# Four layer norms in a two-layer decoder step: the shifted subtraction and all row sums on VectorE, the convolution's history behind the first group's norm

## The chip, the cores and the metric

The kernel runs on one core of one Trainium2 chip. The metric is device time in microseconds (us). Each version is timed in several runs, of which the median is given; beside these one execution is recorded by the hardware profiler, and all times of single instructions come from that one. Engines: PE is the matrix engine (TensorE), PEld its weight loads, DVE is VectorE, ACT is ScalarE, POOL is GpSimd, SP is the engine that issues most DMA transfers. On-chip memory has two parts: SBUF, and PSUM, whose banks receive the results of matmuls.

## The reference

One inference step of a hybrid decoder with two layers, model width 1024, for a new sequence of 512 tokens and 8 single tokens that continue cached sequences. Layer 0 mixes tokens by sliding-window attention, layer 1 by gated linear attention. After each mixer comes a gated feed-forward network with a causal convolution of width 3, and after each of the four sublayers a normalisation of the sum of input and sublayer:

```python
def layer_norm(x, g, b):
    mu = jnp.mean(xf, -1, keepdims=True)
    var = jnp.mean(jnp.square(xf - mu), -1, keepdims=True)
    return (xf - mu) * lax.rsqrt(var + LN_EPS) * g + b

def conv_ffn(x, buf, w_up, conv_w, conv_b, w_down):
    h = x @ w_up
    a, u = h[..., :D_FF], h[..., D_FF:]                  # gate and value, D_FF = 2816
    ap = jnp.concatenate([buf, a], axis=1)               # two rows of history ahead
    c = conv_b + sum(conv_w[j] * ap[:, j:j + T] for j in range(CONV_W))
    return (gelu(c) * u) @ w_down, ap[:, T:]

for i in range(2):
    x = layer_norm(ALPHA * x + mixer_i(x), ln_mix_g[i], ln_mix_b[i])
    f, new_buf = conv_ffn(x, buf, ffn_w_up[i], ffn_conv_w[i], ffn_conv_b[i], ffn_w_down[i])
    x = layer_norm(ALPHA * x + f, ln_ffn_g[i], ln_ffn_b[i])
```

The outputs are the activations, the new keys and values, the new linear-attention states and the new convolution history.

## The kernel before

**Tiling.** Activations stay on the chip, transposed: 128 partitions of features, 8 chunks (`KD = 8`) of the width, tokens along the free dimension. The 520 tokens go as two groups: `a` with 256 tokens, `b` with 264 (256 of the sequence and the 8 single ones). Weights and activations are float32, split into a high and a low part for the matrix engine, so that a product of one weight unit (a 128-column slice of a weight matrix) with one group is three matmuls of each of 8 chunks: high by high (L238), high by low (L240), low by high (L242). Such a product fills one PSUM bank, a tile named `accp`; there are four of these, and a product can start only when the reader of the product four places earlier has emptied its bank. Weight units arrive by DMA in a tile `raw`; ACT makes the high part `wh` (L196), DVE the low part `wl` (L202), or in the feed-forward phases ACT and a DMA issued by POOL (L207, L208).

**A norm.** There are four norms: norm 0 behind the attention, at about 127 to 186 us of the profiled span, norm 1 behind the first feed-forward network (465 to 530 us), norm 2 behind the linear attention (700 to 770 us), norm 3 at the end (1040 to 1092 us). Each is made for group `a` and for group `b`, and group `b`'s products run on PE while group `a` is normalised. `ln_chunk` is called for each of the 8 output chunks, as its product comes: DVE adds the product to the scaled residual (L343 behind the mixers; L337 with a bias behind the feed-forward networks), which empties the product's bank. Behind chunk 0 a matmul with ones gives the mean of that chunk alone (L347), ACT copies it into SBUF in one or two scalings (`sb`, L349; `sa`, L353), and this shift is subtracted from all eight chunks (L356) before the other products are added, so that the later sum of squares is of small numbers. Chunk 0 is subtracted by DVE and chunks 1 to 7 by POOL, one instruction each, so that chunk m's L343 waits for POOL's m-th subtraction. Then ACT squares each chunk (L361), and the sums over the chunks are gathered in `s1` (L373) and in `s2` (L374). Who adds is set by two limits, `p1, p2`: for group `a`, and for both groups in the last norm, DVE adds into `s1` and POOL adds the first three squares into `s2` (m from 1 to 3, `S2P = 4`), DVE the rest; for group `b` in norms 0 to 2 POOL adds all of both but the last. `ln_end` reduces `s1` and `s2` over the partitions by matmuls (L381), has DVE subtract the rest of the mean in pairs of chunks (L403), computes the reciprocal root, and scales each chunk (L441); ACT and DVE then split the result into its high part `xh` (L442) and low part (L443; for group `a` both sit in the tile `xs_a`), which the next products read.

**The feed-forward network's start.** `ffn_open` runs when the first weight unit of the phase is loaded, well ahead of the norm. It issues the DMA of the convolution's history (`sconv`, L760) on ACT's queue, and has POOL compute from it `base`, the history's share of the convolution for the 8 single tokens, in five instructions (L776 to L780). `base` is read by DVE in `ffn_gate` for group `b` (L810). The first four pairs of gate and value units go one by one: `ffn_gate` makes the convolution's taps (L804 on ACT, L805 and L806 on DVE) and the gelu (L815), `ffn_value` multiplies by the value product (L823), which empties that product's bank, and splits the result. When group `b`'s norm ends, the row sums for the next norm are prepared on DVE (L477 to L488).

**The order of the work.** The program is written as a list of slots: each slot is one product of one group, with what belongs to it. Work that should come later is put on a heap with a number of slots to wait (`spawn`, drawn by `due` after each slot). A scheduler with a timeline simulation then sets the order of the instructions on each engine from their dependences and its own costs, so that a change in one place can move instructions in others; `issue_after` adds an order between two instructions. At run time each engine works through its own list in order.

## Time and profile before

| | |
|---|---|
| median of 3 runs | 1097.64 us (1096.99, 1097.64, 1100.53) |
| profiled execution | 1094.2 us, of which the span of instructions is 1092.5 us |
| PE busy | 1059.4 us, 97% of the span |
| DVE busy | 871.7 us, 80%, 1813 instructions |
| ACT busy | 683.4 us, 63% |
| POOL busy | 319.8 us, 29%, 512 instructions |

The profile's page gives the busy time of each engine. Other views used below: the list of waits (which instruction waited for which, with total, times and longest), the timeline of one engine (start and duration of each instruction, with the idle time before it and what ended that), the table of stretches (busy time of each engine in each), the instructions of one source line (duration as least, median and longest), and the chain of waits that leads to the end. A row of the timeline such as "x4" merges four instructions in a row of one kind; its duration is then that from the first start to the last end. A duration includes the time until the result is written, so the next instruction starts before it is over.

### The profile page before, as it was taken

What the parts mean: (1) busy time and instruction counts of PE and PEld (TensorE: products, weight loads), DVE (VectorE), ACT (ScalarE), POOL (GpSimd) and SP (SyncE); (2) the same over time, 40 slices, a digit from 0 to 9 for tenths busy, and PEclk for the clock granted to TensorE, in tenths of its full rate; (3) what the DMA queues carried; (4) which work ended last, traced back from release to release, by engine and by line L of the source; (5) the groups of instructions that cost most, each with busy time, mean ns of one, the idle gap of its engine ahead of it and who ended that gap; (6) DMA issues with size and microseconds to landing.
All of it is one profiled execution on the core that took longest, in us unless ns stands there. A gap on an engine that the chain in (4) does not pass through costs nothing. (4 is left out here: it accounts for less than half of the span.)

```text
span 1092.5 us, 23877 instructions
## 1 busy us (share of the span) xinstructions
PE 1059.4 (97%) x9174; PEld 1030.2 (94%) x9174; DVE 871.7 (80%) x1813; ACT 683.4 (63%) x1356; POOL 319.8 (29%) x512
## 2 busy tenths in 40 slices
PE   8999999999999999999999999989999999999996
PEld 8998899999999999999899999889999999999995
DVE  7898668988778878978767676588988788778975
ACT  5677657776655665547566656468776655665643
POOL 4576572221111110274321111363221111110263
PEclk9999999999999999999999999999999999999998
DMA  7454048587777774448235445368488777774322
GB/s 231 147 170 130 21 121 214 135 216 191 180 177 180 176 176 117 116 139 205 67 103 174 131 149 163 96 172 220 125 216 193 184 174 176 175 189 117 109 74 79
DMA packets 65474, 167.45 MB, mean 153 GB/s; under 512 B 8104, under 2 KB 28624, under 8 KB 65360
## 3 DMA queue, kind: packets, MB, share of 16 engines
q1 hardware_dynamic: 50960, 119.47, 33.8%
q0 software_dynamic: 12240, 44.57, 23.2%
q10 hardware_dynamic: 2160, 1.89, 0.5%
q8 instruction: 72, 1.18, 0.4%
q14 instruction: 42, 0.34, 0.1%
HBM read 153.24 MB, written 8.47 MB: 148 GB/s over the span
## 5 line engine op out<-in xcount | busy, mean ns | idle before, releaser
L315 ACT ACTIVATE wh<-raw 128x1024 fp32r<-128x1024 f32 x72 | 76.0, 1058 | 89.9 <-PE widep L929 44.7
L196 ACT ACTIVATE wh<-raw 128x1024 fp32r<-128x1024 f32 (+1 forms) x92 | 96.2, 1047 | 41.4 <-PE accp L240 14.5
L311 PE MATMUL widep<-tl,wh 128*128 128x264 f32 (+1 forms) x432 | 119.1, 276 | 0.0
L312 PE MATMUL widep<-th,wl 128*128 128x264 f32 (+1 forms) x432 | 119.1, 276 | 0.0
L310 PE MATMUL widep<-th,wh 128*128 128x264 f32 (+1 forms) x432 | 119.1, 276 | 0.0
L238 PE MATMUL accp<-xh_b,wh 128*128 128x264 f32 x400 | 112.9, 282 | 2.7 <-DVE hprod L823 2.7
L242 PE MATMUL accp<-xh_b,wl 128*128 128x264 f32 x400 | 111.4, 279 | 0.0
L208 POOL DMA_DIRECT2D wl<-in_w_down x28 | 24.2, 866 | 291.8 <-ACT wl L207 269.1
L238 PE MATMUL accp<-xs_a,wh 128*128 128x256 f32 x400 | 105.5, 283 | 4.0 <-ACT wh L196 3.3
L240 PE MATMUL accp<-xl_b,wh 128*128 128x264 f32 x384 | 107.0, 279 | 0.0
L240 PE MATMUL accp<-xs_a,wh 128*128 128x256 f32 x384 | 102.5, 282 | 0.0
L316 DVE TENSOR_TENSOR wl<-raw,wh 128x1024 fp32r<-128x1024 f32 x72 | 87.7, 1221 | 7.0 <-ACT wh L315 7.0
L202 DVE TENSOR_TENSOR wl<-raw,wh 128x1024 fp32r<-128x1024 f32 (+2 forms) x64 | 78.8, 1239 | 14.3 <-ACT wh L196 13.0
L207 ACT ACTIVATE wl<-wh 128x1024 fp32r<-128x1024 f32 x85 | 89.0, 1051 | 0.9
L310 PEld LDWEIGHTS widep<-th,wh 128*128 128x128 f32 x432 | 82.1, 190 | 0.0
L311 PEld LDWEIGHTS widep<-tl,wh 128*128 128x128 f32 x432 | 82.1, 190 | 0.0
L312 PEld LDWEIGHTS widep<-th,wl 128*128 128x128 f32 x432 | 82.1, 190 | 0.0
L238 PEld LDWEIGHTS accp<-xs_a,wh 128*128 128x128 f32 x400 | 76.5, 194 | 5.5 <-ACT wh L196 3.8
L238 PEld LDWEIGHTS accp<-xh_b,wh 128*128 128x128 f32 x400 | 75.7, 189 | 4.7 <-DVE hprod L823 3.5
L310 PE MATMUL widep<-xh_b,wh 128*128 128x264 f32 x288 | 79.6, 276 | 0.0
L311 PE MATMUL widep<-xl_b,wh 128*128 128x264 f32 x288 | 79.5, 276 | 0.0
L312 PE MATMUL widep<-xh_b,wl 128*128 128x264 f32 x288 | 79.5, 276 | 0.0
(423 smaller groups left out, 4008.7 us busy)
## 6 DMA issues: line engine op xcount, KB each, us to landing
raw<-in_w_up SPq DMA_DIRECT2D x88, 512.0 KB, 4.0
wl<-in_w_up POOLq DMA_DIRECT2D x52, 512.0 KB, 6.9
raw<-in_w_down SPq DMA_DIRECT2D x44, 512.0 KB, 3.6
wl<-in_w_down POOLq DMA_DIRECT2D x28, 512.0 KB, 6.5
raw<-in_w_gla SPq DMA_DIRECT2D x24, 512.0 KB, 3.5
raw<-in_w_mix_o SPq DMA_DIRECT2D x16, 512.0 KB, 4.1
qs<-hl SPq DMA_DIRECT2D x64, 64.0 KB, 2.1
sgla<-in_state_gla SPq DMA_DIRECT2D x16, 256.0 KB, 3.1
```

The lines of the kernel that those rows point to most:

```text
L196: nc.scalar.activation(h[:, c], r[:, c], AF.Copy)
L202: nc.vector.tensor_tensor(l[:, c], r[:, c], h[:, c].bitcast(F32), op=ALU.subtract)
L207: self.nc.scalar.activation(l, h.bitcast(F32), AF.Copy, scale=-1.0)
L208: self.nc.gpsimd.dma_start(out=l, in_=src, accum_op=ALU.add)
L238: nc.tensor.matmul(o, h[:, ks], xh, start=k == 0, stop=False)
L240: nc.tensor.matmul(o, h[:, ks], xl, start=False, stop=False)
L242: nc.tensor.matmul(o, l[:, ks], xh, start=False, stop=not tail and k == nt - 1)
L310: self.nc.tensor.matmul(o, h[:, ks], rh, start=k == 0, stop=False)
L311: self.nc.tensor.matmul(o, h[:, ks], rl, start=False, stop=False)
L312: self.final = self.nc.tensor.matmul(o, l[:, ks], rh, start=False, stop=k == KD // 2 - 1).ins
L315: self.nc.scalar.activation(hi, src, AF.Copy)
L316: self.nc.vector.tensor_tensor(lo, src, hi.bitcast(F32), op=ALU.subtract)
```

## The change

Three things are changed, in the norms and at the start of the feed-forward networks.

First, the shift is subtracted by DVE alone: chunk 0 as before, then chunks 1 and 2, 3 and 4, 5 and 6 in three instructions of two chunks each, and chunk 7 in one. Second, every addition into `s1` and `s2` is on DVE; the limits are gone. Third, the DMA of the history and POOL's five instructions move from `ffn_open` into a generator of their own, which is put on the heap with three slots to wait (`BASE = 3`), and the DMA is issued on ACT's queue behind the last high part of the norm of the group that was written last (`self.high`; by then that of group `a`).

```diff
-S2P = 4
+BASE = 3
...
-            for i in range(KD):
-                eng = nc.gpsimd if i else nc.vector
-                eng.tensor_tensor(x[:, i], x[:, i], sa if i else sb, op=ALU.subtract)
+            nc.vector.tensor_tensor(x[:, 0], x[:, 0], sb, op=ALU.subtract)
+            for i in range(1, KD, 2):
+                xp = x[:, i:min(i + 2, KD)]
+                nc.vector.tensor_tensor(xp, xp, sa.unsqueeze(1).broadcast_to([P, xp.shape[1], n]), op=ALU.subtract)
...
-        p1, p2 = (KD - 1, KD - 1) if g.i and not last else (0, S2P)
-        (nc.gpsimd if m < p1 else nc.vector).tensor_tensor(g.s1, x[:, 0] if m == 1 else g.s1, x[:, m], op=ALU.add)
-        (nc.gpsimd if m < p2 else nc.vector).tensor_tensor(g.s2, g.s2, q, op=ALU.add)
+        nc.vector.tensor_tensor(g.s1, x[:, 0] if m == 1 else g.s1, x[:, m], op=ALU.add)
+        nc.vector.tensor_tensor(g.s2, g.s2, q, op=ALU.add)
...
-            nc.scalar.activation(g.xh[:, m], parted(x[:, m]), AF.Identity, bias=bi(m))
+            self.high = nc.scalar.activation(g.xh[:, m], parted(x[:, m]), AF.Identity, bias=bi(m)).ins
...
-        nc.scalar.dma_start(out=self.sconv, in_=self.I["state_conv"][layer])
...
+        self.spawn(self.ffn_base(layer), BASE)
+
+    def ffn_base(self, layer):
+        nc = self.nc
+        with self.tc.issue_after(self.high):
+            nc.scalar.dma_start(out=self.sconv, in_=self.I["state_conv"][layer])
+        w = ...
+        b = ...
+        t = self.cp.tile([P, NT - 256], F32, name="hprod", bufs=2)[:, :NF * NS].rearrange("p (j s) -> p j s", j=NF)
+        g = nc.gpsimd
         g.tensor_tensor(self.base, self.sconv[:, :, :, 0], w(0), op=ALU.mult)
         g.tensor_tensor(t, self.sconv[:, :, :, 1], w(1), op=ALU.mult)
         g.tensor_tensor(self.base, self.base, t, op=ALU.add)
         g.tensor_tensor(self.base, self.base, b, op=ALU.add)
         g.tensor_copy(self.nconv_s[:, :, :, 0], self.sconv[:, :, :, 1])
+        yield from ()
```

Counted in the program (each kind of instruction once per place): POOL goes from 517 to 410 instructions, DVE from 1797 to 1880; ACT, PE and SP keep their numbers. In the changed kernel the lines shift: L356 becomes L355 (chunk 0) and L358 (the rest), L343 becomes L344, L373 and L374 become L374 and L375, L403 becomes L404, L441 and L443 become L442 and L444, L823 becomes L831, and L776 to L780 become L783 to L787.

The order on the engines moves with it. The first place is the start of group `a`'s norm 0 on DVE. Before (`hl_b` and `pr` belong to the attention of group `b`, which is still running):

```order
L732 COPY pts<-tp 128x128
L356 TENSOR_TENSOR x_a<-x_a,sb 128x256
L674 RECIPROCAL small<-small 128x2
L343 SCALAR_TENSOR_TENSOR x_a<-x_a,accp 128x256
L676 TENSOR_TENSOR pr<-pr,small 128x2x128
L373 TENSOR_TENSOR s_a<-x_a 128x256
```

and in the changed kernel:

```order
L733 COPY pts<-tp 128x128
L355 TENSOR_TENSOR x_a<-x_a,sb 128x256
L358 TENSOR_TENSOR x_a<-x_a,sa 128x512 x3
L358 TENSOR_TENSOR x_a<-x_a,sa 128x256
L675 RECIPROCAL small<-small 128x2
L344 SCALAR_TENSOR_TENSOR x_a<-x_a,accp 128x256 x4
```

All four subtractions now stand between chunk 0's own and the first addition of a later product (chunk 1's). In the other three norms they stand at the same place.

The second place is the gate stage behind norm 0 on DVE, where the taps and products of group `a` and the end of group `b`'s norm share the engine. Before:

```order
L806 SCALAR_TENSOR_TENSOR conv<-aext,par,conv 128x256
L823 TENSOR_TENSOR hprod<-conv,accp 128x256
L414 SCALAR_TENSOR_TENSOR pv<-sc,r 128x264
L823 TENSOR_TENSOR hprod<-conv,accp 128x256
L441 SCALAR_TENSOR_TENSOR x_b<-x_b,par,pv 128x264 x8
L316 TENSOR_TENSOR hs_a<-hprod,hs_a 128x2x128 x2
L443 SCALAR_TENSOR_TENSOR xl_b<-x_b,par,xh_b 128x264
```

and in the changed kernel:

```order
L831 TENSOR_TENSOR hprod<-conv,accp 128x256
L814 SCALAR_TENSOR_TENSOR conv<-aext,par,conv 128x256
L410 SCALAR_TENSOR_TENSOR sc<-sc,r 128x264
L415 SCALAR_TENSOR_TENSOR pv<-sc,r 128x264
L442 SCALAR_TENSOR_TENSOR x_b<-x_b,par,pv 128x264 x8
L317 TENSOR_TENSOR hs_a<-hprod,hs_a 128x2x128
L444 SCALAR_TENSOR_TENSOR xl_b<-x_b,par,xh_b 128x264
```

The multiplication of the second pair, which stood ahead of group `b`'s scaling, is no longer there: it comes after all eight low parts and most of the row sums, as row 342 of DVE's list where the first stands in row 323. The third place is POOL ahead of group `b`'s share of norm 0. Before:

```order
L374 TENSOR_TENSOR s_a<-s_a,sq 128x256 x2
L799 MEMSET aext 128x2
L469 TENSOR_TENSOR step<-par 128x4
L799 MEMSET aext 128x2
L776 TENSOR_TENSOR base<-sconv,par 128x176
L777 TENSOR_TENSOR hprod<-sconv,par 128x176
L780 COPY sconv<-sconv 128x176
L778 TENSOR_TENSOR base<-base,hprod 128x176
L356 TENSOR_TENSOR x_b<-x_b,sa 128x264 x7
```

and in the changed kernel, where the history follows weight transfers (L209) and small copies of the gate stage:

```order
L209 DMA wl<-in_w_up 128x1024
L320 COPY hist<-aext 128x2
L783 TENSOR_TENSOR base<-sconv,par 128x176
L784 TENSOR_TENSOR hprod<-sconv,par 128x176
L787 COPY sconv<-sconv 128x176
L785 TENSOR_TENSOR base<-base,hprod 128x176
L786 TENSOR_TENSOR base<-base,par 128x176
```

The five history instructions thus leave the stretch between the two groups' norms and come behind seven of the feed-forward phase's weight transfers.

More of the change, by code (lines that the diff above doesn't have):

```diff
@@ L765, in ffn_open @@
         self.nconv_p = p.tile([P, NF, 2], F32, name="nconv_p")
-        w = lambda j: self.par[:, C_CW + (layer * 3 + j) * NF:C_CW + (layer * 3 + j + 1) * NF].unsqueeze(2).broadcast_to([P, NF, NS])
-        b = self.par[:, C_CB + layer * NF:C_CB + (layer + 1) * NF].unsqueeze(2).broadcast_to([P, NF, NS])
         self.pp, self.pp_cm = self.open(f"pair{layer}")
@@ L771, in ffn_open @@
         self.cp, self.cp_cm = self.open(f"chain{layer}")
-        t = self.cp.tile([P, NT - 256], F32, name="hprod", bufs=2)[:, :NF * NS].rearrange("p (j s) -> p j s", j=NF)
         g = nc.gpsimd
@@ L775, in ffn_open @@
         g.tensor_scalar(self.back, self.par[:, b0:b0 + KD], ALPHA, 0.0, op0=ALU.mult, op1=ALU.add)
+        self.spawn(self.ffn_base(layer), BASE)
[3 more added lines that the diff above has]
+            nc.scalar.dma_start(out=self.sconv, in_=self.I["state_conv"][layer])
+        w = lambda j: self.par[:, C_CW + (layer * 3 + j) * NF:C_CW + (layer * 3 + j + 1) * NF].unsqueeze(2).broadcast_to([P, NF, NS])
+        b = self.par[:, C_CB + layer * NF:C_CB + (layer + 1) * NF].unsqueeze(2).broadcast_to([P, NF, NS])
+        t = self.cp.tile([P, NT - 256], F32, name="hprod", bufs=2)[:, :NF * NS].rearrange("p (j s) -> p j s", j=NF)
+        g = nc.gpsimd
         g.tensor_tensor(self.base, self.sconv[:, :, :, 0], w(0), op=ALU.mult)
```

## The prediction

> **What bounds the kernel now.** I read the page's busy times first, then PE's waits, then the table of stretches around the four norms.
>
> ```profile
> PE 1059.4 (97%) x9174; PEld 1030.2 (94%) x9174; DVE 871.7 (80%) x1813; ACT 683.4 (63%) x1356; POOL 319.8 (29%) x512
> ```
>
> ```profile
> PE accp L238 <- ACT wh L196: 3.3, 3, 2.1
> PE accp L238 <- DVE hprod L823: 2.7, 4, 1.3
> PE pv L381 <- DVE s_a L374: 1.8, 1, 1.8
> PE accp L240 <- DVE hl_b L316: 1.2, 1, 1.2
> ```
>
> ```profile
> 125.00:186.00 61.00, 57.98 (x505) 55.14 (x502) 44.66 (x97) 42.71 (x87) 37.46 (x57) 1.00 0.58 149
> 465.00:530.00 65.00, 61.98 (x528) 60.57 (x527) 52.17 (x104) 39.34 (x75) 32.62 (x41) 1.00 0.54 148
> 700.00:770.00 70.00, 64.58 (x540) 61.95 (x538) 56.71 (x130) 48.44 (x97) 34.00 (x54) 1.00 0.61 160
> 1040.00:1082.00 42.00, 41.58 (x350) 40.30 (x348) 30.49 (x54) 18.43 (x37) 22.93 (x28) 1.00 0.17 57
> 1082.00:1093.00 11.00, 0.00 (x0) 0.00 (x0) 5.75 (x11) 3.52 (x7) 4.71 (x7) 0.66 0.29 99
> ```
>
> PE sets the time: 1059.4 of the span of 1092.5, so 33.1 us are idle. Of these 10.5 lie behind the last matmul (the last row: PE 0.00 from 1082 to 1092.5). PE's count of instructions is the same after the change, so only idle time can be won. In the four norm stretches it is 61 - 57.98 = 3.0, 3.0, 5.4 and 0.4 us, 11.9 in all: no gain by the norms can be above that, and much of it has other causes (the wh wait of 2.1 and the gate stage's hprod waits stand in it). A loss has no such ceiling: whatever makes a PSUM bank come free later is new PE idle time. The third column of busy times is DVE's: it has 16.3, 12.8, 13.3 and 11.5 us free in these stretches.
>
> **The change part by part.** *The amount on DVE.* Per norm and group four subtractions are new there; the additions are 3 for group a, 12 for group b in norms 0 to 2, 3 in norm 3. That is 8 x 4 + 4 x 3 + 3 x 12 + 3 = 83, which is the difference 1880 - 1797. Prices, from DVE's timeline of norm 0 and the instructions of lines 373 and 374:
>
> ```profile
> 157.13 2.47 DVE L403 TENSOR_TENSOR x_a<-x_a,tp 128x512 f32<-128x512 f32 x4
> 159.52 0.42 DVE L407 TENSOR_TENSOR sc<-sc,r 128x256 f32<-128x256 f32 x1
> 159.85 0.42 DVE L343 SCALAR_TENSOR_TENSOR x_b<-x_b,accp 128x264 f32<-128x264 f32 x1
> 160.19 0.42 DVE L409 SCALAR_TENSOR_TENSOR sc<-sc,r 128x256 f32<-128x256 f32 x1
> L373 DVE TENSOR_TENSOR s_a<-s_a,x_a x23: 412/545/948, 131.6 to 1061.6; 128x256 f32<-128x256 f32 x23
> L374 DVE TENSOR_TENSOR s_a<-s_a,sq x15: 412/848/2903, 137.7 to 1062.1; 128x256 f32<-128x256 f32 x15
> ```
>
> Four subtractions of two chunks take 2.47 us, so one is 0.60 of the queue (L403 reads one input from PSUM; of two SBUF inputs and this size the trace has none). A single chunk takes the queue 0.34 (159.52 to 159.85 to 160.19). Four subtractions are 3 x 0.60 + 0.34 = 2.14. Group a adds 2.14 + 3 x 0.34 = 3.2 us per norm, group b 2.14 + 12 x 0.34 = 6.2, in norm 3 again 3.2. Norms 0 to 2 add 9.4 each, norm 3 6.4, together 34.6. All of it fits the free time above (9.4 under 12.8). Uncovered it would cost up to 34.6; that end I exclude, since PE's work covers it. What DVE gives back: the same additions run at 412 ns at best but at medians of 545 and 848, so (0.545 - 0.412) x 23 + (0.848 - 0.412) x 15 = 9.6 us of these two groups is slowing while POOL works beside. I price the additions at 0.34, as POOL will be nearly empty there; at the contended 0.95 the 51 additions would take 31 us more, which would still mostly fit.
>
> *The wait that gets longer.* Where the program waits for DVE in this stage is chunk 1. Its update empties the bank that a later product needs, and until now it waited for a single POOL subtraction. In the changed order all four DVE subtractions stand ahead of it. The rows are DVE's chunk 0 subtraction, chunk 1's update, and PE's product that takes the bank, in norms 0 to 3:
>
> ```profile
> 127.76 0.43 DVE L356 TENSOR_TENSOR x_a<-x_a,sb 128x256 f32<-128x256 f32 x1
> 128.85 0.42 DVE L343 SCALAR_TENSOR_TENSOR x_a<-x_a,accp 128x256 f32<-128x256 f32 x1
> 129.32 0.38 PE L238 MATMUL accp<-hs_a,wh 128*128 128x256 f32 x1
> 471.57 0.43 DVE L356 TENSOR_TENSOR x_a<-x_a,sb 128x256 f32<-128x256 f32 x1
> 472.62 0.48 DVE L337 SCALAR_TENSOR_TENSOR x_a<-x_a,back,accp 128x256 f32<-128x256 f32 x1 [0.62 <-POOL x_a L356]
> 473.63 0.28 PE L238 MATMUL accp<-hh_b,wh 128*128 128x264 f32 x1
> 702.25 0.43 DVE L356 TENSOR_TENSOR x_a<-x_a,sb 128x256 f32<-128x256 f32 x1
> 703.41 0.42 DVE L343 SCALAR_TENSOR_TENSOR x_a<-x_a,accp 128x256 f32<-128x256 f32 x1 [0.73 <-POOL x_a L356]
> 703.88 0.38 PE L238 MATMUL accp<-hh_b,wh 128*128 128x264 f32 x1 [0.19 <-DVE x_a L343]
> 1045.76 0.42 DVE L356 TENSOR_TENSOR x_a<-x_a,sb 128x256 f32<-128x256 f32 x1
> 1046.81 0.48 DVE L337 SCALAR_TENSOR_TENSOR x_a<-x_a,back,accp 128x256 f32<-128x256 f32 x1 [0.63 <-POOL x_a L356]
> 1047.82 0.28 PE L238 MATMUL accp<-hh_b,wh 128*128 128x264 f32 x1
> ```
>
> Norm 0: subtractions from 127.76 take 0.34 + 2.14, so chunk 1's update begins at 130.24 and ends at 130.66; PE started 0.05 us behind the old end (128.85 + 0.42 = 129.27), so it starts 1.4 late. Norm 1: 471.57 + 2.48 + 0.48 = 474.53 against 473.63, 0.9 late. Norm 2: 702.25 + 2.48 + 0.42 = 705.15, 1.3 late. Norm 3: 1045.76 + 2.48 + 0.48 = 1048.72, 0.9 late. Together 4.5. But norm 2 has a wait shortly behind whose end PE doesn't set:
>
> ```profile
> 712.87 0.38 PE L240 MATMUL accp<-hl_b,wh 128*128 128x264 f32 x1 [1.16 <-DVE hl_b L316]
> ```
>
> It takes up to 1.16 of the 1.3. So I put the loss at 1.4 + 0.9 + 0.15 + 0.9 = **+3.35**. Its bounds: 0, if every delay meets a wait behind it, and 4.5.
>
> *The stall that goes.* In norm 2 group a's last addition of squares stands between POOL's additions for group b and the history:
>
> ```profile
> 727.37 2.90 DVE L374 TENSOR_TENSOR s_a<-s_a,sq 128x256 f32<-128x256 f32 x1 [0.54 <-ACT sq L361]
> 728.11 0.99 POOL L374 TENSOR_TENSOR s_b<-s_b,sq 128x264 f32<-128x264 f32 x1
> 728.80 0.73 POOL L776 TENSOR_TENSOR base<-sconv,par 128x176 f32<-128x176 f32 x1
> 730.33 0.70 PE L381 MATMUL pv<-s_a,ones_a 128*128 128x256 f32 x2 [1.76 <-DVE s_a L374]
> ```
>
> It takes 2.90 instead of 0.41 while POOL runs without a gap, and PE stands 1.76 for it. Both neighbours are gone after the change. At 0.41 the addition would end 2.5 earlier, so the stall goes: **-1.7** (bounds -1.76 and 0, if squares now come later behind the additions queued ahead). The Trainium skill, page "SBUF — State Buffer", section "Who interferes with whom", has a rule for this: a DVE instruction with two SBUF inputs shares a port pair with a GpSimd instruction that reads SBUF, and the loser is blocked for the whole instruction. This trace agrees, with 2.90 against 0.41 (its 0.41 without POOL is the least of line 374 above). By that rule the stall of 1.76 goes whole.
>
> *Smaller stalls near the norms.*
>
> ```profile
> 139.32 0.38 PE L238 MATMUL accp<-hh_b,wh 128*128 128x264 f32 x1 [0.48 <-ACT hh_b L315]
> 171.43 0.71 PE L381 MATMUL tp<-s_b,ones_a 128*128 128x264 f32 x2 [0.49 <-DVE s_b L373]
> ```
>
> The second is group b's contended sum in norm 0; I let it and the first go: **-0.5 and -0.5** (0 at the other end of each, since other work may move in).
>
> *The gate stage behind norms 0 and 2.* Nothing is added there, but the order shown above delays the second pair's multiplication.
>
> ```profile
> 181.65 0.41 DVE L823 TENSOR_TENSOR hprod<-conv,accp 128x256 f32<-128x256 f32 x1
> 193.28 0.46 DVE L823 TENSOR_TENSOR hprod<-conv,accp 128x256 f32<-128x256 f32 x1
> 193.80 0.38 PE L238 MATMUL accp<-xh_b,wh 128*128 128x264 f32 x1 [1.29 <-DVE hprod L823]
> 185.00:195.00 10.00, 8.71 (x77) 8.52 (x77) 9.84 (x31) 4.55 (x13) 0.81 (x4) 1.00 0.15 30
> ```
>
> DVE is full there (9.84 of 10), and PE already waits for it at 193.80. The second pair's multiplication moves from 181.65 to about where the third now is, 193. The sum of DVE's work up to the later products is unchanged, so I take only a little: **+0.3** per layer, 0.6 (bounds 0 and 1.9 per layer, priced below). *The history:* before, POOL waited for its transfer ahead of group b's subtractions of norm 0:
>
> ```profile
> 141.23 0.49 POOL L776 TENSOR_TENSOR base<-sconv,par 128x176 f32<-128x176 f32 x1 [3.32 <-DMA sconv<-in_state_conv]
> ```
>
> It now costs POOL the same five instructions in the gate stage, behind weight transfers and copies, where POOL has 0.81 of 10 us busy: **0**. Without that cover the reader of `base` on DVE would wait, up to the same 3.3 us.
>
> *Sum:* +3.35 - 1.7 - 0.5 - 0.5 + 0.6 = **+1.25**. The profiled execution of 1094.2 (span 1092.5 and 1.7 around it) would become 1095.45. It lies 3.4 under the median of the runs, so I add the difference to the median: 1097.64 + 1.25 = **1098.9**, which is 0.11% and no change: a measurement of this kernel tells 0.3%, 3.3 us.
>
> **The rivals.** *A, relief wins (faster).* Late banks cost little, since PE arrives late at waits that others end, as at 712.87; and DVE, no longer slowed beside POOL, is earlier at all the waits where PE stands for it: losses 0.6, gains 1.7 + 1.0 and the 2.7 of the hprod waits. That is -4.8: 1092.8. For it speak 9.6 us of slowing in two groups alone; against it that POOL has only 0.81 of 10 us in the stretch of the longest hprod wait, so that this wait isn't contention. The rule of the skill named above is on its side: by it work taken off POOL lets DVE's two-input instructions run alone.
>
> *B, the gate stage blocks (slower).* The second pair's bank is held until about 193.7, and products queued in order on PE wait for it. PE then loses some 1.4 us where it waits 1.29 now and 0.5 behind it, per layer 1.9, and never gets it back: 3.8 in place of my 0.6. With the bank losses at 3.35 and gains of 2.7 the sum is +4.45: 1102.1. It decides from the point at which PE has fewer matmuls of other banks than fill the time to that multiplication. For it speaks DVE's 9.84 of 10; against it that PE's stall at 193.80 is the same one, moved, so that the two need not add.
>
> *C, the history is late.* POOL's weight transfers wait for ACT, and `base` is read by DVE in the gate stage of group b: if POOL has to wait for the later transfer as long as before, 3.3 us, and only then, DVE and PE lose that in each layer: +1.25 + 6.6, 1105.5. POOL's 0.81 of 10 speaks against it: the five instructions have room to be late.
>
> **How the numbers follow.** My forecast 0.44, A 0.32, B 0.20, C 0.04. The forecast's own range is 1095.5 to 1102, from the ends of the bank term and of the smaller stalls. No change is between 1094.3 and 1100.9: of my case 0.34 lies in it, 0.07 above and 0.03 under; of A 0.05, of B 0.05. So faster 0.03 + 0.27 = 0.30, same 0.34 + 0.05 + 0.05 = 0.44, slower 0.07 + 0.15 + 0.04 = 0.26. The range from 1092 to 1103 takes in A's and B's times and leaves out some 0.1 on each side.
>
> **What would show it.** In the changed profile: PE waits of about 1.4, 0.9, 1.3 and 0.9 us for DVE's chunk-1 update, at the first product behind it in each norm (right for the banks); none of over 0.3 us at L381 in norm 2; the additions at a median near 0.41; DVE's busy time up by 15 to 30 us, POOL's down by 75 to 100. PE waits for hprod above 2.7 in sum speak for B, under 1 for A. I am wrong if PE's idle time changes by more than 3.3 us, or if the change sits in a phase without a norm, where only the order of instructions differs.

## The result: about 1% slower, and the profile after

The changed kernel takes 1108.63 us, the median of six runs (1100.78 to 1114.38); the kernel before, run beside it, 1096.97 (1093.86 to 1100.53). The ratio is 1.010 with a 95% interval of 1.0078 to 1.0123. The forecast was 1098.9 in a range of 1092 to 1103: it missed on the slow side. The profiled execution of the changed kernel is its fastest, 1100.78 us, of which the span is 1099.0.

That spread is the first thing to see. Each run also records the mean clock that TensorE was granted:

| run of the changed kernel, us | 1100.78 | 1104.37 | 1106.11 | 1111.15 | 1111.43 | 1114.38 |
|---|---|---|---|---|---|---|
| mean granted clock | 0.996 | 0.994 | 0.990 | 0.986 | 0.984 | 0.984 |

From the first to the last the clock falls by 1.2% and the time grows by 1.2%. The runs of the kernel before had a mean clock of 0.993 to 0.995 in each of the four sets of experiments below. So the loss has two parts: 6.6 us that the profiled execution shows at an undisturbed clock (1100.78 - 1094.2), and some 5 us more in the median, in runs whose clock was lower (the six have a mean of 0.989).

The busy times of the changed kernel (busy us, share of the span, instructions):

```profile
PE 1058.2 (96%) x9174; PEld 1029.7 (94%) x9174; DVE 884.8 (81%) x1896; ACT 685.4 (62%) x1356; POOL 232.1 (21%) x405
```

DVE has 13.1 us more than before, POOL 87.7 less; PE's work is the same, so its idle time grew with the span. The table of stretches says where. First the kernel before, three stretches between norms, which the prediction did not show (from:to, length, then busy time and instructions of PE, weight loads, DVE, ACT and POOL, the granted clock, DMA share and rate):

```profile
186.00:465.00 279.00, 277.21 (x2464) 276.30 (x2463) 237.42 (x425) 174.63 (x263) 44.94 (x91) 1.00 0.67 164
530.00:700.00 170.00, 169.82 (x1411) 159.42 (x1409) 113.79 (x310) 102.43 (x269) 33.13 (x31) 1.00 0.43 136
770.00:1040.00 270.00, 269.07 (x2393) 268.32 (x2392) 228.76 (x397) 170.63 (x254) 42.98 (x81) 1.00 0.69 170
```

and the changed kernel, the same stretches and those of norms 0 to 2:

```profile
125.00:186.00 61.00, 56.32 (x492) 54.06 (x491) 48.58 (x119) 42.15 (x87) 11.08 (x23) 1.00 0.56 140
186.00:465.00 279.00, 276.29 (x2459) 275.71 (x2458) 237.33 (x423) 175.51 (x263) 46.95 (x93) 1.00 0.68 165
465.00:530.00 65.00, 60.87 (x515) 59.17 (x514) 54.59 (x126) 39.09 (x75) 7.96 (x15) 1.00 0.54 148
530.00:700.00 170.00, 167.95 (x1402) 159.79 (x1401) 114.57 (x308) 101.27 (x265) 31.71 (x31) 1.00 0.42 136
700.00:770.00 70.00, 64.37 (x527) 59.50 (x525) 56.89 (x146) 47.15 (x96) 10.63 (x16) 1.00 0.64 165
770.00:1040.00 270.00, 267.85 (x2386) 267.65 (x2387) 227.13 (x403) 172.34 (x255) 46.95 (x89) 1.00 0.69 166
```

Idle PE is the length less the first busy time. Norms 0, 1 and 2 went from 3.0, 3.0 and 5.4 us to 4.7, 4.1 and 5.6: together only 3.0 more. Another 3.9 came in the stretches between norms: 1.8 to 2.7 behind norm 0, 0.2 to 2.05 in the linear attention (530 to 700 us, where no instruction was changed), 0.9 to 2.15 behind norm 2. The clock column reads 1.00 everywhere: none of this is the clock.

PE's waits in the changed kernel (total us, times, longest):

```profile
PE accp L243 <- DMA wl<-in_w_up: 3.7, 2, 2.1
PE accp L239 <- DVE x_a L344: 3.2, 2, 1.7
PE accp L246 <- DMA wl<-in_w_up: 1.9, 3, 1.0
PE accp L239 <- DVE x_a L338: 1.8, 2, 0.9
PE accp L239 <- DVE hprod L831: 1.7, 2, 1.4
PE tp L1234 <- DVE sg L1238: 0.9, 1, 0.9
```

The rows for `x_a` are the bank wait of the prediction: the product waits for DVE to empty its bank, once in each norm. PE's timeline has the four products:

```profile
130.51 0.38 PE L239 MATMUL accp<-hs_a,wh 128*128 128x256 f32 x1 [1.72 <-DVE x_a L344]
130.73 0.28 PE L241 MATMUL accp<-hs_a,wh 128*128 128x256 f32 x1
130.84 0.28 PE L243 MATMUL accp<-hs_a,wl 128*128 128x256 f32 x1
...
475.29 0.35 PE L239 MATMUL accp<-hh_b,wh 128*128 128x264 f32 x1 [0.88 <-DVE x_a L338]
709.45 0.38 PE L239 MATMUL accp<-hh_b,wh 128*128 128x264 f32 x1 [1.51 <-DVE x_a L344]
1054.07 0.35 PE L239 MATMUL accp<-hh_b,wh 128*128 128x264 f32 x1 [0.88 <-DVE x_a L338]
```

1.72, 0.88, 1.51 and 0.88 us. And in the linear attention, the chain of waits runs through a store and a load of the same small buffer (start, duration, what):

```profile
684.64 4.28 DMA out_gla_s<-sgla
688.93 2.66 DMA sgla<-in_state_gla
691.59 0.86 DVE sgla L1207 x2
692.45 0.41 DVE sg L1238
692.91 0.44 PE tp L1234 x2
```

Read so, a head's new state is stored from `sgla` (4.28 us), the next head's old state is then loaded there (2.66), DVE updates a state with `sg` queued behind that, and PE stands 0.9 for `sg`. The last experiment tests this reading, and the reading fails.

### The profile page after: what moved, and what is told of

Read it like the earlier page. It is cut to its first block, busy times and chain, and to the rows that moved or that the text cites. A ratio compares the mean times of both kernels' runs of the same rounds, so it can differ in the third digit from the quotient of the medians.

```text
span 1099.0 us, 23786 instructions
## 1 busy us (share of the span) xinstructions
PE 1058.2 (96%) x9174; PEld 1029.7 (94%) x9174; DVE 884.8 (81%) x1896; ACT 685.4 (62%) x1356; POOL 232.1 (21%) x405
## 4 chain that ended last, share of the span: by engine, by line
PE 77%; DVE 8%; DMA 5%; ACT 5%; issue 2%; POOL 2%; SPq 1%; DVEq 0%; POOLq 0%; ACTq 0%
PE widep L313 9%; PE widep L311 9%; PE widep L312 9%; PE accp L239 8%; PE accp L241 8%; PE accp L243 7%; PE widep L937 5%; PE widep L934 5%; PE widep L936 5%; PE accp L954 2%; DMA wl<-in_w_up 2%; PE onep L313 1%; PE onep L312 1%; PE onep L311 1%; DMA qs<-hl 1%
## 5 line engine op out<-in xcount | busy, mean ns | idle before, releaser
L209 POOL DMA_DIRECT2D wl<-in_w_down x28 | 24.3, 867 | 287.2 <-ACT wl L208 275.0
L858 DVE TENSOR_TENSOR merged<-widep,conv 128x528 f32<-128x528 f32 x72 | 37.4, 561 | 57.0 <-PE widep L313 56.9
```

## The experiments

Ratios are to the kernel before, run on the same chip in the same set. Where a profiled execution had stretches at a low clock, I also give a clock-corrected time of the last matmul against that of the kernel before: from each microsecond the part that the granted clock fell short of full was taken away. That is arithmetic of mine on one execution each, and it counts the whole shortfall as lost, also where PE stood idle; by it the changed kernel is 6.3 us late.

### Which part of the change costs the time

Four kernels. The subtraction on DVE alone (`sub_only`):

```diff
 # the kernel before, with
-            for i in range(KD):
-                eng = nc.gpsimd if i else nc.vector
-                eng.tensor_tensor(x[:, i], x[:, i], sa if i else sb, op=ALU.subtract)
+            nc.vector.tensor_tensor(x[:, 0], x[:, 0], sb, op=ALU.subtract)
+            for i in range(1, KD, 2):
+                xp = x[:, i:min(i + 2, KD)]
+                nc.vector.tensor_tensor(xp, xp, sa.unsqueeze(1).broadcast_to([P, xp.shape[1], n]), op=ALU.subtract)
```

> The subtraction alone on VectorE; sums and history as before. Bank theory: PE waits for DVE's chunk-1 update of about 1.7, 0.9, 1.5 and 0.9 us in norms 0 to 3, as in the changed kernel, and the time is 4 to 6 us above the kernel before in the profiled span. Rival 1 (the loss comes from the sums or the history): within 1.5 us of before and no such waits. Rival 2 (a lower granted clock makes most of it): the instructions of the profile lose little, but the runs spread from about 1100 to 1114 as those of the changed kernel did (clock 0.996 to 0.984).

The row sums on DVE alone (`sums_only`):

```diff
 # the kernel before, with
-        (nc.gpsimd if m < p1 else nc.vector).tensor_tensor(g.s1, x[:, 0] if m == 1 else g.s1, x[:, m], op=ALU.add)
-        (nc.gpsimd if m < p2 else nc.vector).tensor_tensor(g.s2, g.s2, q, op=ALU.add)
+        nc.vector.tensor_tensor(g.s1, x[:, 0] if m == 1 else g.s1, x[:, m], op=ALU.add)
+        nc.vector.tensor_tensor(g.s2, g.s2, q, op=ALU.add)
```

> Both sums alone on VectorE; subtraction on GpSimd and history as before. Bank theory: no waits for the chunk-1 update above 0.3 us, the 1.76 us stall at the reduction of group a's sums in norm 2 is gone or under 0.5; -2 to +1 us against before. Rival 1 (VectorE is loaded too much by the 51 additions): 3 us or more slower. Rival 2 (clock): spread like that of the changed kernel.

The history alone (`hist_only`):

```diff
 # the kernel before, with
-        nc.scalar.dma_start(out=self.sconv, in_=self.I["state_conv"][layer])
...
+        self.spawn(self.ffn_base(layer), BASE)
```

> The move of the convolution history alone. Bank theory: within 2 us of before, the norm-2 stall of 1.76 smaller. Rival (the gate stage: the moved transfer and its five GpSimd instructions delay the low parts of the weights): 2 to 4 us slower, with PE waits for the transfer of wl at about 189, 201, 766 and 779 us as in the changed kernel.

The whole change, with only chunks 0 to 2 shifted at once and the other three subtractions held behind chunk 2's update (`pair_first`):

```diff
 # the changed kernel, with
-            for i in range(1, KD, 2):
-                xp = x[:, i:min(i + 2, KD)]
-                nc.vector.tensor_tensor(xp, xp, sa.unsqueeze(1).broadcast_to([P, xp.shape[1], n]), op=ALU.subtract)
+            g.sa = sa
+            self.shift_pair(g, 1)
...
+        if m == 2:
+            with self.tc.issue_after(upd.ins):
+                for i in range(3, KD, 2):
+                    self.shift_pair(g, i)
```

> The whole change, but only chunk 0 and the pair of chunks 1 and 2 are subtracted ahead of the updates of chunks 1 and 2; the other three subtractions are held behind the update of chunk 2. The chunk-1 update should then end at about 0.34 + 0.60 + 0.42 = 1.36 us behind the start of chunk 0's subtraction, where the kernel before had 1.51 in norm 0. Bank theory: the four waits (1.7, 0.9, 1.5, 0.9) fall under 0.3 each, and the profiled time falls by 3 to 4 us against the changed kernel's 1100.8. Rival (the waits only cover others): they go, but the time stays within 1.5 us of the changed kernel. Clock rival: the runs still spread to about 1114.

| kernel | median, us | ratio, 95% interval | mean clock | last matmul, clock-corrected |
|---|---|---|---|---|
| subtraction alone | 1101.48 | 1.0045 (1.0030 to 1.0060) | 0.992 | +2.3 |
| sums alone | 1094.97 | 0.9986 (0.9971 to 1.0002) | 0.992 | -4.5 |
| history alone | 1096.57 | 0.9990 (0.9973 to 1.0007) | 0.994 | +0.1 |
| whole, one pair ahead | 1104.76 | 1.0063 (1.0038 to 1.0088) | 0.988 | +2.7 |
| (kernel before) | 1096.24 | | 0.994 | |

The subtraction is the one part that costs by itself; the history costs nothing. The three add to 1.002, though, and the whole is 1.010, so parts of it work on one another. The sums alone have a bank wait too, 2.1 us in norm 2, where their expectation was none above 0.3. By the corrected time they are 4.5 us early, and their clock is lower (0.9916 for 0.9941 in the mean of the runs), which is 2.7 us: of what the sums win on PE the clock takes back more than half. With one pair ahead the bank wait goes from norms 0, 1 and 3 (norm 2's is left with 1.5 us, below, from the list of waits), and the loss is 0.6% in place of 1.0%, with intervals that just touch; the corrected time falls from 6.3 to 2.7. So the bank wait is probably a cause, and not the only one; the wait alone, below, tests it without the rest of the change.

```profile
PE accp L239 <- DVE hprod L838: 3.3, 2, 1.8
PE accp L243 <- DMA wl<-in_w_up: 3.0, 1, 3.0
PE accp L239 <- DVE x_a L348: 1.5, 1, 1.5
```

The profile of the subtraction alone shows what the profile of the changed kernel hides. Norm 0 has the same wait of 1.72 us behind the same sequence of matmuls. Its product in PE's timeline:

```profile
130.01 0.58 PE L238 MATMUL accp<-hs_a,wh 128*128 128x256 f32 x1 [1.72 <-DVE x_a L343]
130.38 0.42 PE L240 MATMUL accp<-hs_a,wh 128*128 128x256 f32 x1
```

and its stretches, where the third column from the right is the clock:

```profile
129.20:136.00 6.80, 5.99 (x28) 5.99 (x29) 5.65 (x15) 1.58 (x4) 3.06 (x5) 0.50 0.01 2
132.00:134.00 2.00, 2.00 (x11) 2.00 (x11) 1.93 (x4) 0.42 (x1) 0.99 (x2) 0.50 0.00 0
136.20:139.00 2.80, 2.06 (x19) 1.80 (x20) 1.09 (x4) 1.08 (x4) 1.00 (x5) 1.00 0.00 0
```

From 129.2 us, 0.9 us into the wait, to 136.0 PE's clock was at one half: 11 matmuls in 2 us. In the changed kernel's profiled execution the wait of 1.72 is followed by matmuls 0.11 us apart (130.73, 130.84), at full clock. So one and the same wait is followed by half clock in one execution and not in the other, and one profile can't tell how often. The Trainium skill (page "TensorE: Matmul & The Clock Gate", section "Part 1: The HAM clock gate") has TensorE's clock set to one half or to full by how busy the engine was in windows of about 3.4 us that run freely; 0.50 and a length of 6.8 us, twice 3.4, agree with that, and so does a result that differs between executions. Its section "HAM oscillation — how this bites in real kernels" asks for no idle gaps above about 3.4 us. Here the clock fell within a wait of 1.72 us, with 0.6 us of idle time shortly ahead of it, so the measurement decides for a shorter gap.

### Is it the wait as such, and what do the other pairs of parts give

`wait_only` is the kernel before, with nothing of the change: four idle DVE instructions of the size of a pair, which change no value, stand between chunk 0's subtraction and the updates of group `a`. That is a larger dose than the change's own (waits of 11.8 us, below, for 5.0):

```diff
 # the kernel before, with
+            if g.i == 0:
+                with self.tc.issue_after(sub.ins):
+                    for _ in range(DOSE):                # DOSE = 4
+                        g.hold = nc.vector.tensor_tensor(x[:, 6:8], x[:, 6:8], x[:, 6:8], op=ALU.max).ins
...
+        if m and g.i == 0:
+            stack.enter_context(self.tc.issue_after(g.hold))
```

> The kernel before with nothing moved, but four idle VectorE instructions of two chunks (the larger of a value and itself, in place) between chunk 0's subtraction and the updates of the other chunks of group a, in all four norms: the added wait alone. Bank theory with the clock: PE waits of 1.5 us or more for the chunk-1 update in each norm, 4 to 8 us more time, and a mean granted clock lower than before's by 0.002 or more. Rival 1 (waits there are absorbed later): within 2 us of before. Rival 2 (the clock has nothing to do with waits): time up by the sum of the waits, clock as before.

The changed kernel again (`after_again`, no edit):

> The changed kernel again, on the chip of these comparisons, with a second profile. If its time is 1% above before here too and its runs have a mean granted clock of 0.984 to 0.99 where before has 0.992 to 0.997, the clock is part of its loss; the profile should then show stretches of some 3.4 us at a clock of 0.5 right behind PE's waits near the norms, as the profiles of the four kernels above do and the first profile of the changed kernel (clock 0.996) did not. If instead the ratio falls to 1.005 with the same clock as before, the first measurement was of a worse chip.

Subtraction and sums, with the history as it was (`no_hist`):

```diff
 # the changed kernel, with
+        nc.scalar.dma_start(out=self.sconv, in_=self.I["state_conv"][layer])
...
-        self.spawn(self.ffn_base(layer), BASE)
... # POOL's five instructions go back into ffn_open with it
```

> Subtraction and sums on VectorE, history as before. The parts alone gave +0.45% (subtraction), -0.14% (sums) and -0.1% (history), +0.2% as a sum against 1.0% of the whole. If the parts add, this is +0.3% and the whole loss needs the history; if subtraction and sums disturb each other (VectorE's order in the gate stage), it is +0.7% or more here already, with PE waits for transfers of wl at about 189, 201 and 779 us; if the history disturbs, those waits are missing.

Sums and history, with the subtraction as it was (`sums_hist`):

```diff
 # the changed kernel, with
-            nc.vector.tensor_tensor(x[:, 0], x[:, 0], sb, op=ALU.subtract)
-            for i in range(1, KD, 2):
-                xp = x[:, i:min(i + 2, KD)]
-                nc.vector.tensor_tensor(xp, xp, sa.unsqueeze(1).broadcast_to([P, xp.shape[1], n]), op=ALU.subtract)
+            for i in range(KD):
+                eng = nc.gpsimd if i else nc.vector
+                eng.tensor_tensor(x[:, i], x[:, i], sa if i else sb, op=ALU.subtract)
```

> Sums on VectorE and history moved, the subtraction left on GpSimd. Bank theory: no waits for the chunk-1 update above 0.3 us and the time -0.5 to 0% against before, so that the subtraction is the only part that loses. Rival (the history with emptied GpSimd makes the low parts of the weights late): +0.3% or more.

| kernel | median, us | ratio, 95% interval | mean clock | last matmul, clock-corrected |
|---|---|---|---|---|
| wait alone | 1111.97 | 1.0134 (1.0114 to 1.0154) | 0.987 | +5.3 |
| changed kernel again | 1106.03 | 1.0101 (1.0060 to 1.0141) | 0.992 | +6.3 |
| subtraction and sums | 1106.34 | 1.0085 (1.0068 to 1.0101) | 0.990 | +4.8 |
| sums and history | 1097.26 | 0.9999 (0.9983 to 1.0016) | 0.991 | -1.5 |
| (kernel before) | 1097.97 | | 0.993 | |

The wait alone makes the kernel 1.3% slower. Its list of waits:

```profile
PE accp L239 <- DVE x_a L332: 6.6, 2, 3.3
PE accp L239 <- DVE x_a L333: 3.5, 1, 3.5
PE tp L698 <- DVE pr L689: 1.7, 1, 1.7
```

The first two rows are the bank wait in norms 1 to 3; in norm 0 PE has other work there, and waits 1.7 us for `pr`, which stands behind the idle instructions. These are 11.8 us of waits, for a loss of 14.7 in the median (1.0134 x 1097 - 1097). Of that only 5.3 us are in the corrected time; the lower clock (0.987 for 0.993) makes up most of the rest. In its profile a stretch at half clock begins in each of the four waits or right behind it. The one in norm 1 (stretches of 2 us, as above):

```profile
476.00:478.00 2.00, 0.00 (x0) 0.00 (x0) 1.93 (x3) 0.00 (x0) 2.00 (x2) 1.00 0.98 370
478.00:480.00 2.00, 0.77 (x5) 0.80 (x6) 2.00 (x5) 0.81 (x2) 2.00 (x4) 0.89 0.05 18
480.00:482.00 2.00, 2.00 (x11) 2.00 (x11) 1.93 (x4) 0.42 (x1) 1.92 (x3) 0.50 0.00 0
```

PE stands still, and then makes 11 matmuls in 2 us. A stretch of 3.4 us at a clock of 0.50 costs half of itself, 1.7.

The changed kernel's second profile was again at a clock of 0.996, with one stretch of 3.4 us at half clock, from 746.5 us on, behind none of its bank waits. Its slower runs (clock 0.986 and 0.989) have no profile.

Of the two pairs that were run, the one with the subtraction loses (1.0085), and the whole change without the subtraction doesn't (0.9999). Subtraction with sums loses more than the subtraction alone, though the sums alone lose nothing. Corrected for the clock, 7 us lie between the sum of the two (2.3 - 4.5) and the pair (4.8). By the same arithmetic at the norms' first subtractions, 1.8 of them arise between norm 1 and norm 2, 0.9 in norm 2 and 2.7 between norm 2 and norm 3. The instructions of the linear attention, which lies in the first of these, are the same in all these kernels, in another order; that the order makes the difference is my reading, and not shown.

### Does it go when PE is kept busy

`fill_wait` is the kernel with the wait alone, and TensorE gets idle work in the wait, matmuls of ones whose result nobody reads. `fill_after` is the changed kernel with fewer of them (FILL 14 and 4):

```diff
 # wait_only, and the changed kernel, with
+            if g.i == 0:
+                for _ in range(FILL):
+                    nc.tensor.matmul(mp[:, :P], self.ones_a, self.ones_a, start=True, stop=True)
```

> The kernel with the added waits alone, and 14 matmuls of ones with ones into the bank of the mean, whose result nobody reads, behind group a's mean: they stand right ahead of the product that waits some 3.3 us in norms 1 to 3, and should take about 0.21 us each, 3.0 in all, out of the waiting time. Clock theory (an idle PE, not the waiting itself, makes the clock fall): the stretches at 0.5 right behind these three products are gone, the granted clock is up by 0.003 or more from 0.9865, and the time falls by 3 to 5 us from 1.0134 of before, to 1.009 to 1.0105, although PE does more and the products start no earlier. Rival (the clock falls for another reason, such as the load of VectorE or chance): clock and time as without the fill, or slower by the fill.

> The changed kernel with 4 such matmuls (0.85 us) ahead of the four products that wait 1.7, 0.9, 1.5 and 0.9 us. Clock theory: the waits for the chunk-1 update shrink to about 0.9, 0, 0.7 and 0, products start no earlier, and the runs lie closer to the undisturbed 1100 to 1102: median 1 to 3 us less than the changed kernel's 1.0101 of before. Rival (other waits of PE trigger the clock as well, and these are too short to matter): within 1 us of the changed kernel.

`split` takes the sums of the change, and of the subtraction only chunks 0 to 2; POOL subtracts chunks 3 to 7, and the history is as before. `sums_again` is the sums alone, a second time.

```diff
 # sums_only, with
-            for i in range(KD):
-                eng = nc.gpsimd if i else nc.vector
-                eng.tensor_tensor(x[:, i], x[:, i], sa if i else sb, op=ALU.subtract)
+            nc.vector.tensor_tensor(x[:, 0], x[:, 0], sb, op=ALU.subtract)
+            nc.vector.tensor_tensor(x[:, 1:3], x[:, 1:3], sa.unsqueeze(1).broadcast_to([P, 2, n]), op=ALU.subtract)
+            for i in range(3, KD):
+                nc.gpsimd.tensor_tensor(x[:, i], x[:, i], sa, op=ALU.subtract)
```

> Sums on VectorE, history as before, and of the subtraction only chunk 0 and the pair of chunks 1 and 2 on VectorE, chunks 3 to 7 on GpSimd. The chunk-1 update should come no later than before, and GpSimd, with two subtractions less, frees its own queue 1.6 us earlier. Bank theory: no waits for the chunk-1 update above 0.3 us in norms 0, 1 and 3, and 0.1 to 0.4% faster than before. Rival (the order in the linear attention's end and the gate stage decides, whatever the banks do): anything from -0.2% to +0.6%, with waits there.

> Sums on VectorE alone again, for a tighter interval than 0.9986 (0.9971 to 1.0002). If the sums themselves gain, 0.9975 to 0.9995 again; if that was chance, 1.000 or above.

| kernel | median, us | ratio, 95% interval | mean clock | last matmul, clock-corrected |
|---|---|---|---|---|
| wait alone, PE filled | 1108.07 | 1.0103 (1.0084 to 1.0122) | 0.994 | +9.8 |
| changed, PE filled | 1101.58 | 1.0049 (1.0029 to 1.0069) | 0.990 | +0.6 |
| split subtraction | 1095.36 | 0.9986 (0.9976 to 0.9997) | 0.991 | -5.6 |
| sums again | 1096.24 | 0.9998 (0.9986 to 1.0009) | 0.992 | -3.4 |
| (kernel before) | 1096.46 | | 0.994 | |

With PE filled the kernel with the wait has the clock of the kernel before again, 0.994 against 0.987, and is 0.3% faster although PE has more to do. Norm 1's filler (14 matmuls, which the trace shows as 28 instructions) and product on PE, and the same stretches as above:

```profile
474.20 3.29 PE L373 MATMUL sc<-ones_a 128*128 128x128 f32 x28
477.66 0.35 PE L240 MATMUL accp<-hh_b,wh 128*128 128x264 f32 x1 [0.17 <-DVE x_a L333]
```

```profile
478.00:480.00 2.00, 2.00 (x21) 2.00 (x20) 1.97 (x4) 0.36 (x2) 1.96 (x3) 1.00 0.00 0
480.00:482.00 2.00, 2.00 (x21) 2.00 (x20) 1.93 (x4) 1.54 (x3) 1.59 (x2) 1.00 0.03 8
```

The product starts 3.46 us behind the filler's start, no earlier than behind the wait of 3.27; but then 21 matmuls fit in 2 us in place of 11. None of the four waits, now filled, has a stretch at half clock behind it, and the clocks of the four runs (0.993 to 0.995, for 0.985 to 0.988) don't overlap: that idle PE sets off the half clock is shown by this pair. The clock's part is 0.77% of 1097 (0.9942 - 0.9865) or 8.5 us, and the kernel won only 3.4 by the ratios: four fillers of some 3.3 us are 13.2, for 11.8 us of waits, and the corrected times differ by 4.5 (9.8 - 5.3).

In the changed kernel the filling halves the loss, from 1.010 to 1.005, but not by the clock: that stayed at 0.990. By the corrected times 5.7 us were won, and the stretch of the linear attention shows some 2 us of it:

```profile
530.00:700.00 170.00, 170.00 (x1423) 163.58 (x1423) 116.40 (x310) 102.26 (x266) 30.12 (x31) 0.99 0.43 137
```

PE idles 0.00 us there, against 2.05 in the changed kernel, and nothing in this stretch was edited. From norm 1's subtraction of group `b` to norm 2's of group `a` PE idles 2.83 us in the kernel before (of 219.78), 5.30 in the changed one (of 224.11) and 2.91 in this one (of 221.94). In the linear attention, which no edit touches, what differs is the order of the same instructions; why four fillers undo the loss there isn't shown.

The split subtraction is the one kernel whose interval lies under 1, by 0.14% (0.03 to 0.24): it beats the kernel before by little, and the changed kernel by 1.1%. Its bank waits are 0.5 us in norm 0 and 2.0 in norm 2, none in the other two. The sums alone, over both sets, make no measurable difference; here too the corrected time is early (3.4 us) and the clock low (0.991 for 0.994).

Half clock isn't tied to the waits of the subtraction. In the profiles of the sums alone and the history alone, and in that of the kernel before without a store (below), stretches at half clock stand also behind other waits of PE of some 2 us: for `hh_b`, for `hprod`, for the high part `wh`, for a row sum. So PE's idle time as such sets it off, in some executions, and the kernel before has such waits as well.

### The store in the linear attention

To test the chain of store and load, the store of the third head's state is left out of the changed kernel, and of the kernel before:

```diff
 # the changed kernel (after_nostore), and the kernel before (before_nostore), with
-            nc.sync.dma_start(out=self.O["gla_s"][2 * p:2 * p + 2, h].rearrange("b k v -> k b v"), in_=s)
+            if h != 2:
+                nc.sync.dma_start(out=self.O["gla_s"][2 * p:2 * p + 2, h].rearrange("b k v -> k b v"), in_=s)
```

> The changed kernel without the four stores of the third linear-attention head's state for the single tokens (that part of the output is left out), so that the loads of the last head's state need not wait for a store to land. Store-chain theory: the two PE waits at about 691 and 693 us (for the activation of on and for sg on VectorE, 1.4 to 2.0 us together) are gone, and the kernel is 2 to 4 us faster than the changed kernel: 1.006 to 1.008 of before. Rival (chance of the order: the chain is one of many and another takes its place): 1.009 or more, with other waits in the stage.

> The kernel before without the same four stores (left out likewise). Store-chain theory: no change, 0.999 to 1.001, as nothing waits for these transfers there. Rival (any change of order is worth a few us): a difference of 2 us or more, in either direction.

And eight fillers in norm 2 of the split kernel, whose profile has a low clock there (`split_fill`):

```diff
 # split, with
+            self.means = getattr(self, "means", 0) + 1
+            for _ in range(FILL if self.means == 5 else 0):
+                nc.tensor.matmul(mp[:, :P], self.ones_a, self.ones_a, start=True, stop=True)
```

> The version with the sums on VectorE and the subtraction split between the engines, with 8 matmuls of ones (1.7 us) in norm 2 alone, ahead of the product that waits 2.0 us there for VectorE and behind which the clock stood at 0.5 for 3.4 us. Clock theory: that stretch is gone, mean clock up by 0.0015 from 0.991, and 1 to 2 us less than the split version's 0.9986 of before: 0.997 to 0.9985. Rival: the clock falls at another place instead, 0.9985 to 1.000.

| kernel | median, us | ratio, 95% interval | mean clock | last matmul, clock-corrected |
|---|---|---|---|---|
| changed, without that store | 1107.42 | 1.0093 (1.0069 to 1.0116) | 0.989 | +3.3 |
| before, without that store | 1098.09 | 1.0012 (0.9996 to 1.0028) | 0.994 | +1.1 |
| split, PE filled in norm 2 | 1095.41 | 0.9989 (0.9976 to 1.0003) | 0.992 | -4.5 |
| (kernel before) | 1096.37 | | 0.995 | |

Without the store the changed kernel is not measurably faster than with it (1.0093 against 1.0100 and 1.0101), and PE's wait for `sg` is still there:

```profile
698.92 0.44 PE L1235 MATMUL tp<-ident,on 128*128 128x128 f32 x2 [0.94 <-DVE sg L1239]
```

So the store isn't what this wait needs. The rows ahead of it, first with the store, then without:

```profile
691.03 0.90 ACT L1206 ACTIVATE sgla<-sgla,ep 128x256 f32<-128x256 f32 x2
691.57 0.88 DVE L1207 SCALAR_TENSOR_TENSOR sgla<-vb,kraw,sgla 128x256 f32<-128x256 f32 x2 [1.30 <-DMA sgla<-in_state_gla]
697.05 0.90 ACT L1206 ACTIVATE sgla<-sgla,ep 128x256 f32<-128x256 f32 x2
697.59 0.88 DVE L1207 SCALAR_TENSOR_TENSOR sgla<-vb,kraw,sgla 128x256 f32<-128x256 f32 x2 [1.30 <-ACT sgla L1206]
```

In both DVE idles 1.30 us and starts 0.54 behind ACT's scaling of the state. The first profile puts the wait down to the load that landed at that moment, but the scaling had already read the state by then: DVE waits for ACT, and `sg` stands behind that. The smaller wait ahead of it, 0.47 us for `on`, is gone without the store, and the corrected time is 3.0 us better, by one execution each.

This profile, at a clock of 0.986, is also the nearest thing on record to the changed kernel at a low clock. It has seven stretches of 3.4 us at half clock. One stands behind norm 0's bank wait and three behind waits for low parts of weights in the gate stages, among them:

```profile
131.44 0.43 PE L239 MATMUL accp<-hs_a,wh 128*128 128x256 f32 x1 [1.72 <-DVE x_a L344]
188.62 1.16 PE L246 MATMUL accp<-xs_a,wl 128*128 128x256 f32 x8 [1.90 <-DMA wl<-in_w_up]
786.05 0.38 PE L243 MATMUL accp<-xs_a,wl 128*128 128x256 f32 x1 [2.60 <-DMA wl<-in_w_up]
```

The fillers in norm 2 gave no time: in the split kernel's profile the clock is 0.50 from 708 to 710 us, with them 1.00 there, but 0.61 from 718 to 722.

## Why the prediction was wrong

**The bank term was right.** Forecast were waits of 1.4, 0.9, 1.3 and 0.9 us, 4.5 in all; measured 1.72, 0.88, 1.51 and 0.88, 5.0. DVE's timeline confirms the price of the subtractions:

```profile
127.63 2.43 DVE L358 TENSOR_TENSOR x_a<-x_a,sa 128x512 f32<-128x512 f32 x4
```

The absorption in norm 2 came as well: the wait of 1.16 for `hl_b` is no longer in the list. So the term is about +3.8 (5.0 - 1.2), for +3.35.

**The stall at the row sums went,** as forecast (-1.7): no row sum is among PE's waits of over 0.2 us. The additions, from the instructions of lines 374 and 375 (least, median, longest in ns):

```profile
L374 DVE TENSOR_TENSOR s_a<-s_a,x_a x23: 411/424/428, 132.7 to 1066.4; 128x256 f32<-128x256 f32 x23
L375 DVE TENSOR_TENSOR s_a<-s_a,sq x27: 411/423/426, 132.4 to 1066.9; 128x256 f32<-128x256 f32 x27
```

Their medians fell from 545 and 848 to 424 and 423. That agrees with the rule of the Trainium skill that the prediction cited (page "SBUF — State Buffer", section "Who interferes with whom"). DVE's busy time rose by 13.1 only (15 to 30 forecast). In time it bought nothing: the sums alone are at 0.9986 and 0.9998, since their earlier last matmul (4.5 and 3.4 us, corrected) met a lower clock. Of the two smaller stalls, the one at L381 in norm 0 went; of the other's group a wait of 0.98 for `hh_b` is left, where before there were three of 0.54, 0.20 and 0.48. That is -0.7 for the forecast -1.0.

**The gate stage was sized too small** (+0.6). PE's waits for `hprod` fell from 2.7 to 1.7, as rival A would have it; but PE now waits for the low parts of the weights, 3.7 and 1.9 us (first and third row of its waits) in place of these of the kernel before:

```profile
PE accp L245 <- DMA wl<-in_w_up: 0.6, 2, 0.3
PE accp L242 <- DMA wl<-in_w_up: 0.4, 1, 0.4
```

The first row goes with the moved history and the sums together: it is 4.2 in that pair of parts, 3.0 with one pair ahead, 2.2 in the changed kernel again, and at most 0.7 where one of the two parts is missing. But that pair of parts has 8.3 us of waits for low parts and no loss (0.9999), and the sums alone 3.1, so these rows by themselves don't decide the time. Together with `hprod` they are +3.6.

**The linear attention wasn't in the sum at all.** The prediction named it among what would make it wrong, "a phase without a norm, where only the order of instructions differs", and gave it no amount. It is +1.9 in the profile. The terms as measured, 3.8 - 1.8 - 0.7 + 3.6 + 1.9, make 6.8; the span grew by 6.5. The rows were picked after the event, and smaller ones differ both ways, so part of that agreement is luck. PE's idle time grew by 7.7 us (33.1 to 40.8), more than the 3.3 that the prediction named as a sign of being wrong.

**The steps that failed.** The forecast missed by 9.7 us. Of these 5.3 are in the sum, which made +1.25 where the profile has 6.6: the gate stage at 0.6 for 3.6, and the linear attention at nothing for 1.9. The other 4.4 are in the last step, "It lies 3.4 under the median of the runs, so I add the difference to the median". It takes the difference between one execution and the median as the same for both kernels. For the kernel before it is 3.4 us, for the changed one 7.9 (1108.63 - 1100.78), in runs with a lower clock. That waits of PE are followed, in some executions, by stretches at half clock is shown above; that it is the new waits which lower the changed kernel's mean is shown only for the larger dose of the wait alone. A us of new PE wait was priced at 1 us; there 11.8 us of it cost 14.7.

**The rivals.** A fell: the relief is there (additions, `hprod`), and the time isn't. The sums alone come near it by the corrected time (4.5 us early, for A's 4.8), and not by the measured one. B ended on the right side by the wrong mechanism: its waits for `hprod` were to go above 2.7, and fell. C fell: POOL did wait for the history, longer than feared,

```profile
189.65 1.00 POOL L783 TENSOR_TENSOR base<-sconv,par 128x176 f32<-128x176 f32 x1 [6.13 <-DMA sconv<-in_state_conv]
```

but DVE had to wait for `base` only once, 1.2 us, and the history alone is at 0.999. Its trace may be the first row of waits for low parts, above.

**What stays open:** which of the changed kernel's waits set off the low clock in its own runs (filling group `a`'s waits did not raise its mean, and the profile without the store has most of its stretches behind other waits), why the linear attention's order got worse, and what part of the interaction of subtraction and sums is chance of the scheduler.

## What to carry to other kernels

An instruction moved ahead of the one that frees a PSUM bank can cost the matrix engine idle time even where its new engine has room; move only what that next reader needs (chunks 0 to 2 here), and leave the rest where it was. Where the matrix engine sets the time, allow for new waits to cost more than their length (14.7 us for 11.8 here), and judge a change by several runs with their granted clock, since one profiled execution may show none of the stretches at half clock. In a kernel whose order a scheduler sets, any edit also moves phases that it doesn't touch, here by some 2 us in one phase: put that into the range. Where a profile names one releaser of a wait, leave that one out and look whether the wait goes; here it stayed.

## What the runs showed of the hardware

TensorE waits of 1.7 us (subtraction alone) and 3.3 to 3.5 us (wait alone) were followed by stretches of 3.4 or 6.8 us at a clock of 0.50, each 3.4 us of which costs 1.7 us; the same 1.72 us wait in another execution was followed by full clock. Other waits of some 2 us set off such stretches too, in the kernel before without a store as well (a wait of 2.46 us for a row sum, in norm 2). Idle matmuls in the wait brought the mean clock from 0.987 to 0.994. The run times of the changed kernel spread by 1.2% with their mean clock, 0.996 to 0.984. Additions of two 128x256 SBUF tiles on VectorE had medians of 545 and 848 ns beside GpSimd's work and of 424 and 423 without most of it.
